# Weight casts put behind a stage's modulated tiles, and half of the sums of squares behind attention moved to Pool

## The chip, the cores and the metric

One core of one Trainium2 chip. The metric is the device time of one execution in microseconds (us); the median of three runs is given. The core's engines are TensorE (PE; its weight loads PEld), VectorE (DVE), ScalarE (ACT), Pool (POOL) and SyncE (SP, which issues the loads).

## The reference

Two token streams, 256 latent tokens and 256 context tokens of width 1024, go through two layers. A layer is: half feed-forward, a mixer, half feed-forward. Each block modulates its input with a shift and a scale that depend on a conditioning vector, and ends in a post-norm (residual times a constant, plus the gated output, then a layer norm). The mixer is attention in layer 0 and an mLSTM in layer 1; behind the mLSTM only the latents go on.

```python
def half_ffn(h, shift, scale, gate, w_in, w_out, g, b):
    xm = modulate(h, shift, scale)
    a, u = jnp.split(xm @ w_in, 2, axis=-1)
    y = (jax.nn.silu(a) * u) @ w_out
    return post_norm(h, 0.5 * gate * y, g, b)

for i in range(DEPTH):
    h_lat = half_ffn(h_lat, mod_lat[0], mod_lat[1], mod_lat[2], ...)
    h_ctx = half_ffn(h_ctx, mod_ctx[0], mod_ctx[1], mod_ctx[2], ...)
    xm_lat = modulate(h_lat, mod_lat[3], mod_lat[4])
    xm_ctx = modulate(h_ctx, mod_ctx[3], mod_ctx[4])
    o_lat, o_ctx = attention_mixer(...) if i % N_MIXERS == 0 else mlstm_mixer(...)
    h_lat = post_norm(h_lat, mod_lat[5] * o_lat, ln_g[i, 1], ln_b[i, 1])
    ...
```

## The kernel before, in words

The tokens lie along the free axis, the latents first (LAT, 0 to 256), the context behind them (CTX, 256 to 512); the width 1024 is eight tiles of 128 partitions. A product in nearly full precision is made of three matmuls (mm3): an operand is split into a rounded part and the low part that is left, and rounded x rounded, rounded x low and low x rounded are summed. split (line 225 on ScalarE, line 230 on VectorE) makes the two parts: ScalarE casts the number to its rounded part, then VectorE subtracts that from the number.

Weights come in chunks of 128 x 1024. chunk takes a raw buffer (three in rotation, in some stages one more), issues the load on SP's queue, takes one of seven pairs of buffers and splits. While the stage's function is being written out, a chunk stands where its unit first asks for it; a planner then orders the instructions of each engine by their readiness in its own model and keeps to data dependences, buffers, instructions pinned in order and edges that the kernel adds by hand. behind adds such an edge: if the fence has an entry for the instruction's engine, the instruction is to stand behind that entry's on this engine. Before the change only start uses it.

norm is a generator that writes a layer norm and the modulation of its result a step at a time, called by letters at chosen places: "b" or "B" begins one (latents or context), "m" makes the mean, eight "c" (line 478 subtracts the mean, line 485 squares on ScalarE, line 495 sums the squares), "v" the variance and the root (a chain of small instructions, lines 517 and 261 to 268, then line 521), "r" spreads the root over the partitions by a matmul (line 458, as are those of mean and variance), and eight "x" make the modulated tiles: line 551 on VectorE, the rounded part by line 552 on ScalarE, the low part by line 553 on VectorE. The tables LEADSTEP, ATTSTEP, MLSTEP, TAILSTEP and MTAILSTEP say after which unit and which k a letter is called. Line 495 sums on VectorE, but in the norm ahead of the last feed-forward (alone) on Pool for the tiles in POOLA.

A stage opens while the one before it ends: the norm of the latents is written in the tail of the earlier stage, that of the context in the first units of the new one, which work on the latents alone. In a feed-forward the first four units (LEAD) of two chunks each are first done for the latents, then for the context. In attention a unit is a block of 256 columns (part, two chunks, for one tile of 128 tokens; tokens 0 and 1 are the latents). In the mLSTM (jobs) a unit is one chunk: jobs 0 to 3 are queries and need the latents alone, job 4 the gates, jobs 5 to 8 the keys; jobs 0 to 6 (MLLEAD) are first done for the latents, then jobs 4 to 6 for the context, then 7 and 8 for both. Behind them come the value products (token_product, lines 969 to 971). The lines of the mLSTM that set the order are these:

```python
MLSTEP = {(1, 0): 'mcccccccc', (3, 5): 'v', (3, 7): 'rxxxxxxxx'}
MLLEAD = 7
...
            for n, (ws, i, to) in enumerate(jobs[:MLLEAD]):
                o = product(ws, i, LAT, None, lambda k: self.steps(MLSTEP.get((n, k), "")))
```

For the feed-forward LEADSTEP has the context's "v" at (2, 1) and "rxxxxxxxx" at (2, 5), for attention ATTSTEP has them at (3, 6) and (5, 0), with n counting the calls of part.

Of the kernel before, what the change touches and what calls it, by code (L numbers as in the profile page):

```python
# [54 lines left out]

LEAD = 4
TAIL = 4
ATTU = 4
# [55 lines left out]
FILL = (-1, -1, 1, 7)  # L114

POOLA = (0, 1, 2, 3, 4, 5, 6)
MAGIC = float(0x5F3759DF - (1 << 22))
# [54 lines left out]
class Body:  # L172
# [59 lines left out]
    def behind(self, ins):  # L232

        last = self.fence.get(ins.ins.engine)
        if last is not None:
            edge = mybir.DependencyInfo(mybir.DependencyClass.NoSync, mybir.DependencyReason.DATA)
            self.tc.add_manual_dep(ins.ins, last.ins.name, edge, reason="behind the start")

    def mm3(self, out, w, x, first, last, pin=False, group=True):
# [183 lines left out]

    seven = False

# [28 lines left out]
    def norm(self, g, coef, keep=True, nxt=True, alone=False):  # L454
# [20 lines left out]
        for d in range(ND):  # L475
# [10 lines left out]
            if alone and d in SQA:  # L486
                sums[d] = q, q
                continue
            eng = nc.gpsimd if alone and d in POOLA else V
            if eng not in sums:  # L490
# [51 lines left out]
        for d in range(ND):  # L542
# [8 lines left out]
            V.scalar_tensor_tensor(x, z, c[:, v, d : d + 1], rb[:, :w], ALU.mult, ALU.mult)  # L551
            S.activation(xh, x, AF.Identity, bias=e)  # L552
            V.scalar_tensor_tensor(self.xl[:, d, t0:t1], x, e, xh.bitcast(F32), ALU.add, ALU.subtract)
# [153 lines left out]
    def ffn(self, layer, s, gate, groups, side, start=None):  # L707
        nc, V = self.nc, self.nc.vector
        li = layer * 2 + s
        allg = BOTH  # L710
        call = lambda *k: side.get(k, lambda: None)()
        with self.tc.tile_pool(name=f"ffn{li}", bufs=1) as gp:
# [35 lines left out]
            for hf in range(2):  # L748
                js = list(range(hf * NFH, (hf + 1) * NFH))[0 if hf else done :]
                if hf == 0 and not start:  # L750
# [4 lines left out]
                    k0, k1 = range(ND // 2), range(ND // 2, ND)  # L755
                    for j in first[:-1]:
                        unit_in(j, ws[j], LAT, LEADSTEP[li])
                    j = first[-1]
# [8 lines left out]
                    for j in first:  # L767
                        call("in", j)
                    js = js[LEAD:]
                fast, sums = FAST[li]  # L770
# [203 lines left out]

    def attention(self, gate, side):
        nc, V, S, a = self.nc, self.nc.vector, self.nc.scalar, self.a
        with self.tc.tile_pool(name="att", bufs=1) as gp:
# [159 lines left out]
            for tiles in ((0, 1), (2, 3)):  # L1137
                assert len(self.running) == (tiles == (0, 1))
                for blk in range(3):
                    for tt in tiles:  # L1140
                        part(blk, tt, lambda k: self.steps(ATTSTEP.get((n, k), "")))
                        n += 1
                        if (blk, tt) == (2, 1):

                            for i in tiles:
                                part(3, i, ks=range(ND // 2))
                        if n > FINEATT:
                            self.fine = False
                        if blk == 1 and tt == tiles[1]:
                            done(n, 0, tiles, LAG + (tiles[0] > 0))  # L1150
                        turns(n)
            for tt in range(4):
                part(3, tt, ks=range(ND // 2 if tt < 2 else 0, ND))
# [66 lines left out]
    def mlstm(self, gate, side):  # L1220
        self.seven = True
        nc, V, S, a = self.nc, self.nc.vector, self.nc.scalar, self.a
        with self.tc.tile_pool(name="ml", bufs=1) as gp:
# [39 lines left out]
            outs = []  # L1263
            for n, (ws, i, to) in enumerate(jobs[:MLLEAD]):
                o = product(ws, i, LAT, None, lambda k: self.steps(MLSTEP.get((n, k), "")))
                if n < MH:
# [4 lines left out]
            for n, (ws, i, to) in enumerate(jobs):  # L1271
                if n < MH:
                    continue
                if n < MLLEAD:
                    o = product(ws, i, CTX, outs[n])
# [11 lines left out]
                if i >= MH - 2:  # L1287
                    w_v[0]((i - MH + 2) * ND)
            del w, w_q, w_g, ws, jobs
            wait = []  # L1290
            w_o = Keep(self, [a["ml_o"][i] for i in range(ND)], SH)
# [522 lines left out]
```

## Time and profile before

| | |
|---|---|
| time, median of 3 runs | 1612.9 us (1610.75 to 1613.86) |
| time of the profiled execution | 1613.07 us |
| its span, first to last instruction | 1611.2 us |
| TensorE busy | 1591.7 us, 99% |
| VectorE busy | 1369.2 us, 85% |
| ScalarE busy | 758.0 us, 47% |
| Pool busy | 30.6 us, 2% |
| mean granted clock of TensorE | 0.999 |

A time line of the trace gives the start in us from the first instruction, the time in us, engine and line, the operation with its shape and count, and in brackets the idle time of that engine just before and what ended it. A line of a helper (225, 230, 241) stands for all its callers, so places are told by their time.

### The profile page before, as it was taken

What the parts mean: (1) busy time and instruction counts of PE and PEld (TensorE: products, weight loads), DVE (VectorE), ACT (ScalarE), POOL (GpSimd) and SP (SyncE); (2) the same over time, 40 slices, a digit from 0 to 9 for tenths busy, and PEclk for the clock granted to TensorE, in tenths of its full rate; (3) what the DMA queues carried; (4) which work ended last, traced back from release to release, by engine and by line L of the source; (5) the groups of instructions that cost most, each with busy time, mean ns of one, the idle gap of its engine ahead of it and who ended that gap; (6) DMA issues with size and microseconds to landing.
All of it is one profiled execution on the core that took longest, in us unless ns stands there. A gap on an engine that the chain in (4) does not pass through costs nothing.

```text
span 1611.2 us, 26781 instructions
## 1 busy us (share of the span) xinstructions
PE 1591.7 (99%) x10364; PEld 1443.4 (90%) x10364; DVE 1369.2 (85%) x2790; ACT 758.0 (47%) x1342; POOL 30.6 (2%) x38
## 2 busy tenths in 40 slices
PE   9999999999999999999999999999999999999998
PEld 7888888889988998989999998889999889999986
DVE  7789989879878879689977989689977868897687
ACT  6522123215776444515652535326642757566542
POOL 0000000000011000000000000000000000020000
PEclk9999999999999999999999999999999999999999
DMA  9667877642203352542345252753363333527552
GB/s 361 219 209 225 260 229 243 218 133 86 66 1 105 106 157 67 196 157 105 105 171 183 79 179 70 253 179 106 131 203 112 112 118 92 161 101 262 184 170 92
DMA packets 72832, 250.02 MB, mean 155 GB/s; under 512 B 8952, under 2 KB 11768, under 8 KB 72704
## 3 DMA queue, kind: packets, MB, share of 16 engines
q1 hardware_dynamic: 70944, 246.99, 46.6%
q8 instruction: 81, 1.33, 0.3%
q10 hardware_dynamic: 1616, 0.79, 0.2%
q0 software_dynamic: 144, 0.52, 0.1%
q14 instruction: 47, 0.39, 0.1%
HBM read 247.22 MB, written 1.05 MB: 154 GB/s over the span
## 4 chain that ended last, share of the span: by engine, by line
PE 81%; DVE 10%; DMA 4%; ACT 3%; issue 1%; POOL 0%; DVEq 0%; ACTq 0%; SPq 0%; POOLq 0%
PE t L241 67%; PE t L1499 4%; DVE t L230 3%; PE t L969 2%; DMA t<-in_ffn_last 2%; PE t L970 2%; PE t L971 2%; ACT t L225 1%; DVE t L891 1%; PE t L897 1%; DMA t<-in_ffn_in 1%; DVE t L359 1%; DVE t L887 1%; DMA t<-in_ml_qk 1%; PE t L458 0%
## 5 line engine op out<-in xcount | busy, mean ns | idle before, releaser
L241 PE MATMUL t<-t,t 128*128 128x256 f32 (+2 forms) x8484 | 1299.0, 314 | 8.9 <-ACT t L552 4.2
L241 PEld LDWEIGHTS t<-t,t 128*128 128x128 f32 x8484 | 1175.4, 188 | 119.2 <-ACT t L552 5.2
L225 ACT CAST t<-t 128x512 fp32r<-128x512 f32 (+3 forms) x573 | 435.9, 785 | 507.6 <-PE t L241 187.0
L230 DVE TENSOR_TENSOR t<-t,t 128x256 fp32r<-128x256 f32 (+3 forms) x792 | 514.8, 686 | 95.4 <-ACT t L225 93.8
L359 DVE SCALAR_TENSOR_TENSOR t<-t,t 128x1024 bf16<-128x1024 f32 x224 | 260.5, 1219 | 0.2 <-DMA t<-in_ada_w 0.2
L741 DVE SCALAR_TENSOR_TENSOR t<-t,t,t 128x256 f32<-128x256 f32 x96 | 42.9, 478 | 46.0 <-PE t L241 45.8
L969 PE MATMUL t<-t,t 128*128 128x256 f32 (+1 forms) x256 | 78.8, 310 | 0.4 <-ACT t L552 0.4
L971 PE MATMUL t<-t,t 128*128 128x256 f32 (+1 forms) x256 | 78.4, 308 | 0.0
L970 PE MATMUL t<-t,t 128*128 128x256 f32 (+1 forms) x256 | 78.2, 307 | 0.0
L599 ACT ACTIVATE t<-t 128x256 f32<-128x256 f32 (+1 forms) x67 | 32.2, 483 | 93.7 <-PE t L241 92.4
L897 PE MATMUL t<-t,t 128*128 128x512 f32 (+1 forms) x300 | 60.8, 364 | 0.2 <-DVE t L891 0.2
L897 PEld LDWEIGHTS t<-t,t 128*128 128x128 f32 x300 | 51.4, 189 | 9.5 <-DVE t L891 0.6
L1499 PE MATMUL t<-t,t 128*128 128x512 f32 (+2 forms) x276 | 55.9, 358 | 0.0
L1499 PEld LDWEIGHTS t<-t,t 128*128 128x128 f32 (+1 forms) x276 | 45.0, 183 | 11.2 <-issue 1.5
L653 DVE TENSOR_TENSOR t<-t,t 128x512 f32<-128x512 f32 x78 | 53.5, 685 | 0.7
L969 PEld LDWEIGHTS t<-t,t 128*128 128x128 f32 x256 | 48.2, 189 | 3.3 <-ACT t L552 0.6
L970 PEld LDWEIGHTS t<-t,t 128*128 128x128 f32 x256 | 48.1, 188 | 2.7 <-DVE t L230 0.2
L971 PEld LDWEIGHTS t<-t,t 128*128 128x128 f32 x256 | 48.0, 188 | 2.5
L600 DVE TENSOR_TENSOR t<-t,t 128x256 f32<-128x256 f32 (+1 forms) x67 | 36.3, 544 | 16.1 <-ACT t L599 10.1
L552 ACT ACTIVATE t<-t,t 128x256 fp32r<-128x256 f32 x72 | 32.4, 502 | 37.3 <-DVE t L551 37.3
L890 ACT ACTIVATE t<-t,t 128x1024 fp32r<-128x1024 f32 x22 | 25.1, 1152 | 27.8 <-DVE t L888 26.5
L575 ACT ACTIVATE t<-t,t 128x256 f32<-128x256 f32 x64 | 29.7, 503 | 16.4 <-DVE t L574 16.4
(205 smaller groups left out, 1060.5 us busy)
## 6 DMA issues: line engine op xcount, KB each, us to landing
t<-in_ffn_in SPq DMA_DIRECT2D x168, 512.0 KB, 4.1
t<-in_ada_w SPq DMA_DIRECT2D x138, 512.0 KB, 4.4
t<-in_ffn_out SPq DMA_DIRECT2D x66, 512.0 KB, 4.5
t<-in_ffn_last SPq DMA_DIRECT2D x22, 512.0 KB, 3.7
t<-in_att_in SPq DMA_DIRECT2D x12, 512.0 KB, 3.7
t<-in_att_out SPq DMA_DIRECT2D x8, 512.0 KB, 3.5
t<-in_ml_qk SPq DMA_DIRECT2D x8, 512.0 KB, 4.5
t<-in_ml_v SPq DMA_DIRECT2D x8, 512.0 KB, 4.1
```

The source lines that it names most:

```text
L225: self.behind(self.nc.scalar.copy(h, x))
L230: self.behind(self.nc.vector.tensor_tensor(out=ls, in0=xs, in1=hs.bitcast(F32), op=ALU.subtract))
L241: mm = lambda *k, **kw: self.nc.tensor.matmul(*k, skip_group_check=not group, **kw)
L359: ins = nc.vector.scalar_tensor_tensor(self.tmp().bitcast(BF16), r, 1.0, self.cb[:, v, :], ALU.mult, ALU.mult, accum_out=to)
L600: V.tensor_tensor(out=sl, in0=sl, in1=pu[:, :n], op=ALU.mult)
L653: add = lambda o, x, y: V.tensor_tensor(out=o, in0=x, in1=y, op=ALU.add)
L741: V.scalar_tensor_tensor(z, y[:, gg[0] - t0 : gg[1] - t0], gate()[:, v, d : d + 1], z, ALU.mult, ALU.add)
L897: pin(nc.tensor.matmul(o, gs[g], ws[k][w][:, i : i + n], start=k == k0 and g == w == 0, stop=k == k1 - 1 and g == 1,))
L969: mm(o, self.xh[:, k, c], wh, start=k == 0, stop=False)
L970: mm(o, self.xh[:, k, c], wl, start=False, stop=False)
L971: mm(o, self.xl[:, k, c], wh, start=False, stop=k == ND - 1)
L1499: mm = lambda *k, **kw: pin(nc.tensor.matmul(*k, **kw))
```

## The change

A method hold_back sets the fence to ScalarE's last instruction of line 552 written so far. It is called in the feed-forward's first units ahead of the third unit, in attention ahead of the third block of the first two token tiles, in the mLSTM ahead of job 4 and again ahead of job 8; the fence is cleared at the end of each of these parts. While it is set, each cast that split writes is given an edge to that instruction. The fence has an entry for ScalarE alone, so the low parts on VectorE have none. Second, in the norm of the latents that attention's tail begins, line 495 sums the squares of tiles 2 to 5 on Pool, those of the others on VectorE.

```diff
--- before.py
+++ after.py
@@ -54,6 +54,7 @@
 FILLED = {6: (0, 1, 2), 7: (3, 4, 5)}
 
 LEAD = 4
+BACK = 2
 TAIL = 4
 ATTU = 4
 
@@ -113,6 +114,7 @@
 MLLEAD = 7
 FILL = (-1, -1, 1, 7)
 
+POOLD = (2, 3, 4, 5)
 POOLA = (0, 1, 2, 3, 4, 5, 6)
 MAGIC = float(0x5F3759DF - (1 << 22))
 
@@ -235,6 +237,9 @@
         if last is not None:
             edge = mybir.DependencyInfo(mybir.DependencyClass.NoSync, mybir.DependencyReason.DATA)
             self.tc.add_manual_dep(ins.ins, last.ins.name, edge, reason="behind the start")
+
+    def hold_back(self):
+        self.fence = {self.xlast.ins.engine: self.xlast}
 
     def mm3(self, out, w, x, first, last, pin=False, group=True):
         (wh, wl), (xh, xl) = w, x
@@ -421,7 +426,7 @@
         return ab, s, d
 
 
-    seven = False
+    seven = pooled = False
 
     def add_sum(self, g, d):
 
@@ -486,7 +491,7 @@
             if alone and d in SQA:
                 sums[d] = q, q
                 continue
-            eng = nc.gpsimd if alone and d in POOLA else V
+            eng = nc.gpsimd if d in (POOLA if alone else POOLD if self.pooled and g == LAT else ()) else V
             if eng not in sums:
                 sums[eng] = q, None
             else:
@@ -549,7 +554,7 @@
             xh = self.xh[:, d, t0:t1]
             e = e[:, v, d : d + 1]
             V.scalar_tensor_tensor(x, z, c[:, v, d : d + 1], rb[:, :w], ALU.mult, ALU.mult)
-            S.activation(xh, x, AF.Identity, bias=e)
+            self.xlast = S.activation(xh, x, AF.Identity, bias=e)
             V.scalar_tensor_tensor(self.xl[:, d, t0:t1], x, e, xh.bitcast(F32), ALU.add, ALU.subtract)
             if d == 1 and rs is not None and not raw:
                 S.copy(rs[:, :w], rb[:, :w])
@@ -706,6 +711,7 @@
 
     def ffn(self, layer, s, gate, groups, side, start=None):
         nc, V = self.nc, self.nc.vector
+        self.pooled = False
         li = layer * 2 + s
         allg = BOTH
         call = lambda *k: side.get(k, lambda: None)()
@@ -754,6 +760,8 @@
 
                     k0, k1 = range(ND // 2), range(ND // 2, ND)
                     for j in first[:-1]:
+                        if j == first[BACK]:
+                            self.hold_back()
                         unit_in(j, ws[j], LAT, LEADSTEP[li])
                     j = first[-1]
                     ps = unit_in(j, ws[j], LAT, ks=k0)
@@ -766,6 +774,7 @@
                         unit_in(j, ws[j], CTX)
                     for j in first:
                         call("in", j)
+                    self.fence = {}
                     js = js[LEAD:]
                 fast, sums = FAST[li]
                 w = Stream(self, [w_out[hf * NFH + i] for i in range(NFH)], lambda c, hf=hf: SHR if hf and c == (ND - TAIL) * NFH // ND else 0)
@@ -973,6 +982,7 @@
 
 
     def attention(self, gate, side):
+        self.pooled = True
         nc, V, S, a = self.nc, self.nc.vector, self.nc.scalar, self.a
         with self.tc.tile_pool(name="att", bufs=1) as gp:
             t = lambda shape, dt=F32, **k: self.t(shape, dt, pool=gp, **k)
@@ -1137,6 +1147,8 @@
             for tiles in ((0, 1), (2, 3)):
                 assert len(self.running) == (tiles == (0, 1))
                 for blk in range(3):
+                    if blk == BACK and tiles[0] == 0:
+                        self.hold_back()
                     for tt in tiles:
                         part(blk, tt, lambda k: self.steps(ATTSTEP.get((n, k), "")))
                         n += 1
@@ -1149,6 +1161,7 @@
                         if blk == 1 and tt == tiles[1]:
                             done(n, 0, tiles, LAG + (tiles[0] > 0))
                         turns(n)
+                self.fence = {}
             for tt in range(4):
                 part(3, tt, ks=range(ND // 2 if tt < 2 else 0, ND))
                 n += 1
@@ -1262,6 +1275,8 @@
             jobs = [(w_q, hd, qT) for hd in range(MH)] + [(w_g, 0, None)] + [(w, hd, kT) for hd in range(MH)]
             outs = []
             for n, (ws, i, to) in enumerate(jobs[:MLLEAD]):
+                if n == 2 * BACK:
+                    self.hold_back()
                 o = product(ws, i, LAT, None, lambda k: self.steps(MLSTEP.get((n, k), "")))
                 if n < MH:
                     conv(o, 1, i, qT[:, i, :])
@@ -1271,6 +1286,8 @@
             for n, (ws, i, to) in enumerate(jobs):
                 if n < MH:
                     continue
+                if n == MLLEAD + 1:
+                    self.hold_back()
                 if n < MLLEAD:
                     o = product(ws, i, CTX, outs[n])
                 else:
@@ -1287,6 +1304,7 @@
                 if i >= MH - 2:
                     w_v[0]((i - MH + 2) * ND)
             del w, w_q, w_g, ws, jobs
+            self.fence = {}
             wait = []
             w_o = Keep(self, [a["ml_o"][i] for i in range(ND)], SH)
 
```

## Rows read from the trace of the kernel before

**Rows 1.** the page: busy us (share of the span) xinstructions
```profile
PE 1591.7 (99%) x10364; PEld 1443.4 (90%) x10364; DVE 1369.2 (85%) x2790; ACT 758.0 (47%) x1342; POOL 30.6 (2%) x38
```

**Rows 2.** waits of TensorE: total us, times, longest us
```profile
PE t L241 <- ACT t L552: 4.2, 4, 1.2
```

**Rows 3.** TensorE's timeline, layer 1's first feed-forward: start, us, line, [idle before]
```profile
902.12 4.55 PE L241 MATMUL t<-t,t 128*128 128x256 f32 x37 [1.07 <-ACT t L552]
```

**Rows 4.** timeline of ScalarE, the same stretch
```profile
900.61 1.05 ACT L225 CAST t<-t 128x1024 fp32r<-128x1024 f32 x1 [1.60 <-DMA t<-in_ffn_in]
901.57 1.70 ACT L552 ACTIVATE t<-t,t 128x256 fp32r<-128x256 f32 x4
...
907.66 1.41 ACT L485 ACTIVATE t<-t 128x256 f32<-128x256 f32 x4 [2.53 <-DVE t L478]
```

**Rows 5.** timeline of TensorE, start of attention
```profile
382.38 0.38 PE L969 MATMUL t<-t,t 128*128 128x256 f32 x1 [0.39 <-ACT t L552]
```

**Rows 6.** timeline of TensorE, start of the feed-forward behind attention
```profile
551.42 1.44 PE L241 MATMUL t<-t,t 128*128 128x256 f32 x10 [1.20 <-ACT t L552]
```

**Rows 7.** timeline of VectorE, end of attention
```profile
543.02 0.41 DVE L495 TENSOR_TENSOR t<-t,t 128x256 f32<-128x256 f32 x1
```

**Rows 8.** timeline of ScalarE, end of attention
```profile
541.86 0.41 ACT L485 ACTIVATE t<-t 128x256 f32<-128x256 f32 x1
```

**Rows 9.** line 495 on VectorE and on Pool: ns min/median/max
```profile
L495 DVE TENSOR_TENSOR t<-t,t x56: 409/415/424, 367.1 to 1261.5; 128x256 f32<-128x256 f32 x56
...
L495 POOL TENSOR_TENSOR t<-t,t x6: 741/800/990, 1414.9 to 1419.8; 128x256 f32<-128x256 f32 x6
```

**Rows 10.** timeline of VectorE beside Pool's additions, ahead of the last feed-forward
```profile
1415.32 1.51 DVE L483 SCALAR_TENSOR_TENSOR t<-t,t,t 128x256 fp32r<-128x256 f32 x2
...
1421.01 0.47 DVE L483 SCALAR_TENSOR_TENSOR t<-t,t,t 128x256 fp32r<-128x256 f32 x1
```

**Rows 11.** timeline of ScalarE, start of the mLSTM
```profile
1246.03 1.05 ACT L225 CAST t<-t 128x1024 fp32r<-128x1024 f32 x1
...
1268.03 1.05 ACT L225 CAST t<-t 128x1024 fp32r<-128x1024 f32 x1 [4.29 <-DMA t<-in_ml_qk]
...
1272.50 1.05 ACT L225 CAST t<-t 128x1024 fp32r<-128x1024 f32 x1 [0.79 <-DMA t<-in_ml_qk]
1273.46 1.71 ACT L552 ACTIVATE t<-t,t 128x256 fp32r<-128x256 f32 x4
```

**Rows 12.** timeline of TensorE, start of the mLSTM
```profile
1250.15 3.80 PE L241 MATMUL t<-t,t 128*128 128x256 f32 x31 [0.99 <-ACT t L552]
...
1263.68 3.23 PE L241 MATMUL t<-t,t 128*128 128x256 f32 x26 [1.10 <-DVE t L230]
...
1267.21 5.89 PE L241 MATMUL t<-t,t 128*128 128x256 f32 x47
1274.01 18.02 PE L241 MATMUL t<-t,t 128*128 128x256 f32 x107 [0.92 <-ACT t L552]
1291.88 0.39 PE L969 MATMUL t<-t,t 128*128 128x512 f32 x1
```

**Rows 13.** timeline of VectorE, the context's root in the mLSTM
```profile
1262.63 0.16 DVE L517 TENSOR_SCALAR t<-t 128x2 f32<-128x2 f32 x1
...
1266.39 0.42 DVE L521 TENSOR_TENSOR t<-t,t 128x256 f32<-128x256 f32 x1
```

**Rows 14.** timeline of VectorE, the same steps unfilled, behind attention
```profile
568.46 0.16 DVE L266 TENSOR_TENSOR t<-t 128x2 f32<-128x2 f32 x1
568.65 0.16 DVE L267 SCALAR_TENSOR_TENSOR t<-t,t 128x2 f32<-128x2 f32 x1
```

**Rows 15.** stretches: length, PE busy (matmuls), PEclk, DMA, GB/s
```profile
1603.40:1607.40 4.00, 0.00 (x0) 1.00 0.00 0
1607.50:1611.20 3.70, 0.00 (x0) 0.50 0.39 144
```

**Rows 16.** timeline of SP's queue, start of the mLSTM
```profile
1264.47 0.33 SPq L210 DMA_DIRECT2D t<-in_ml_qk  x1
```

## The prediction

> **What bounds the kernel now.** I read the busy shares first: TensorE's matmuls fill 99% of the span and no other engine is near that [rows 1]. With one core and the matmuls one behind another, an edit can gain only what TensorE stands still, or lose by making it stand still. Second, the waits of TensorE: the largest entry, 4.2 us in four waits, is for ScalarE's line 552, the rounded part of a modulated tile, with which a stage opens [rows 2]. The span less TensorE's busy time is 19.5 us, 1.2% of the run, so no gain here can be large. Third, the timelines at the four places where a stage opens: latents into the feed-forward unit of layer 1, into attention, into the feed-forward unit behind attention, and into the mLSTM.
>
> The clearest is layer 1's first feed-forward. TensorE idles 1.07 us for line 552 until 902.12 [rows 3]. In ScalarE's timeline the reason stands just ahead: at 900.61 it runs a weight cast (line 225) whose load had landed only then (1.60 us idle for DMA), and the six waiting tiles follow from 901.57 [rows 4]. That cast belongs to unit 3; TensorE has units 0 to 2 to do first. ScalarE takes its instructions in order, so a cast that waits for a load holds tiles that are ready.
>
> **The change, part by part.** It has two mechanisms.
>
> *Casts behind the tiles in feed-forward and attention.* hold_back makes every later split's cast stand behind the last tile written by line 552 so far. In both feed-forward units it is called ahead of unit 2, when that is tile 7 of the latents (the context's tiles are emitted at (2, 5), later). In layer 1 the casts of chunks 4 to 6 move behind tile 7. They take 3 x 1.05 us and fill the 2.5 us in which ScalarE idled until 907.66 [rows 4], so they cost nothing; without that cover the context's squares would start about 1 us later. Their low parts, which free the raw buffers and so start SP's next loads, are already behind the tiles on VectorE; no load is later. Gain 1.2 us (the 1.07 of [rows 3] plus restart). Attention opens the same way: 0.39 us of waiting for line 552 [rows 5]; gain 0.5 us. Next late in both is the pace of VectorE's tile pairs, which TensorE does not outrun by more than a few tenths. Bounds for the two together: 0.5 to 2.0 us. Behind attention the casts that move keep no matmul waiting today; nothing.
>
> *Pool sums squares behind attention.* Of VectorE's seven additions (line 495) for the latents, four go, and Pool gets three; the variance takes two more one-column matmuls, under 0.3 us. The stage's stall is 1.20 us of idle until 551.42 [rows 6], at the end of the chain variance, root, spread, tile. The last addition starts at 543.02 [rows 7], but the last square ends at 541.86 + 0.41 [rows 8], so the variance can move forward by at most about 0.75 us, although four additions are up to 1.66 us. An addition takes 0.80 us on Pool against 0.415 on VectorE [rows 9]. The variance now waits for Pool too: its three additions can run from the fourth square on and end about with the last; nothing queues behind them, as Pool has 38 instructions in all [rows 1]. There is also a price: where Pool adds today, ahead of the last feed-forward, two VectorE instructions of line 483 took 1.51 us together, and the one behind them, without Pool beside it, 0.47 [rows 10]. That is an excess of 0.28 us for each, and I take it once per Pool addition: 0.85 lost against 1.66 leaves 0.8, about the 0.75 that the squares allow, and less the extra matmuls a gain of 0.5 us. Bounds: 1.1 us lost (three Pool additions block VectorE wholly, 2.4, and the extra 0.3 is paid, against 1.66) to 1.2 gained (the whole stall).
>
> The Trainium skill (SBUF — State Buffer, section "SBUF: two separate sides") speaks against this part: GpSimd and a VectorE instruction with two SBUF inputs share a port pair as an exclusive lock, the loser waiting for the whole instruction. Rows 10 agree in kind, though not in full length. By the rule taken to its end, the part loses the 1.1 us of the lower bound instead of gaining 0.5, and the sum is 1.6 us higher.
>
> *The mLSTM: the step that decides.* Here hold_back stands ahead of job 4, the gates. But MLSTEP emits the context's tiles, 'rxxxxxxxx', at (3, 7), inside job 3. So the last tile at that moment is the context's tile 7, not the latents'. The casts of jobs 4, 5 and 6 (gates and two key units), today from 1246.03 to about 1252, in the middle of the latents' tiles [rows 11], go behind an activation that ends at 1273.46 + 1.71 = 1275.2 [rows 11]. The second call, ahead of job 8, then adds nothing.
>
> Those three jobs are what TensorE does today while the context is normalised: 26 and 47 matmuls in the stretches from 1263.68 and 1267.21 [rows 12], 73 in all, where three units of 24 are 72. Behind the change it has nothing else: jobs 0 to 3 are done, their remaining products need the same weights, and the value products need loads whose buffers these casts hold. TensorE stands from the end of job 3, near 1260, to the first held-back cast.
>
> When does it go on? From 1275.2 I take off: 1.0 us, the latents' wait for line 552 at 1250.15, gone as in the other stages [rows 12]; 1.9 us, in which casts that wait for loads (1268.03, 1272.50) held the context's tiles [rows 11]; 1.5 us in the chain of the root, which runs 517 to 521 in 3.76 us, each small step filled up by a low part [rows 13], where unfilled steps follow at 0.19 us [rows 14] (eight are 1.6 us, with the convolutions some 2.2). That is 1270.8; one cast of 1.05 later, 1271.8; VectorE has one low part less ahead of the variance, so 1271.5. What then remains is the 73 matmuls (3.23 + 5.89 us), seven more of job 4 (0.8), and the unbroken work from 1274.01 to the first value product at 1291.88 (17.9) [rows 12]: about 27.6 without their tails, to 1299.0. So this stage ends 7.1 us later.
>
> To that comes the clock. In the last two stretches of the span, which have no matmul, the granted clock is 1.00 and then 0.50, 1.2 GHz [rows 15]. The hole, 11 us without work, is longer than both, so I expect the first matmuls behind it at the lower level. No row has matmuls at that level: bounds are nothing, and a whole unit (2.7 us) taking twice its time. I take 2.0 us. SP's three loads, issued today from 1264.47 [rows 16] as low parts free their buffers, come some 8 us later, but job 7 needs its weights only behind the 144 matmuls of jobs 4 to 6, over 16 us; ScalarE's and VectorE's queues behind the casts hold convolutions and gates that shift with TensorE. Bounds for the stage: 4.5 us lost (chain 2 us faster than I take it, no clock) to 12 (chain as late as today, full clock price).
>
> **Sum.** -1.2 - 0.5 - 0.5 + 7.1 + 2.0 = +6.9 us on the profiled execution's 1613.07 us, 0.2 above the median of 1612.9: 1620.0 us.
>
> **Rivals.** *No hole, faster.* If the edge is to the latents' tile, or the planned order still lets jobs 4 to 6 go early, the mLSTM gains instead: the wait until 1250.15 (0.99) and the one until 1274.01 (0.92) [rows 12], with restarts 2.2; total -1.2 - 0.5 - 0.5 - 2.2 = -4.4, 1608.7 us. For it speaks that a second call for job 8 would make sense only then; against it that the order of emission in MLSTEP is explicit and line 225 is fenced by engine. It turns on which tile is last at job 4. 12%.
> *Short hole, level.* If the context's chain, with VectorE and ScalarE freed of casts and low parts, ends near 1268.5 and the clock holds, the loss is 4.5 and the gains reach 3.5: 1614 us, within what can be told. Against it: eight tiles cost VectorE twelve instructions ahead of the last activation however free it is. 13%.
> *Long hole.* The context's chain is no faster than today: 1276.2 to go on, 11.8 us, with 2.7 for the clock 14.5; less 2.2: 1625.4. It is the upper end of my forecast, not counted apart.
>
> **How the numbers follow.** Slower by about 7 us: 75%, its own range 1615 to 1625.5. The measurement can tell 0.2%, 3.2 us, from no change. The forecast and its long end are slower; the short hole is the same; no hole is faster. For 8 in 10 the range takes the forecast and part of the short hole: 1611.5 to 1625.5.
>
> **What would show it.** Right: in the mLSTM stage the three casts stand behind the last eight line-552 activations; one idle piece of TensorE of 8 to 12 us ends with line 225, a clock below 1 behind it; the first value product comes 5 to 12 us later relative to the stage's first matmul. The waits near 902 and 382 are gone, three Pool additions of 0.8 us stand near 540. Wrong: casts of the gates ahead of the context's tiles, or matmuls of jobs 4 to 6 in the hole.

## The result, and the profile after

The changed kernel takes 1618.8 us (median of six runs, 1616.2 to 1620.3), the kernel before 1613.1 in the same session (six runs, 1610.8 to 1614.7): a ratio of 1.0036, 95% interval 1.0023 to 1.0049, or 5.7 us slower. The profiled execution is the fastest of the six, 1616.24 us with a span of 1614.4, so its whole is only 3.2 us above the profile before, and the change's cost has to be read in its stage. Line numbers have moved: the cast 225 is now 227, its low part 230 is 232, mm3 241 is 246, the norm's matmuls 458 are 463, the tile lines 551 to 553 are 556 to 558, 478/485/495 are 483/490/500, 517 is 522, 521 is 526, 969 is 978, and the 483 of [rows 10] is 488. Two lines of VectorE come up beside them: 435, now 440, adds to the running sum for the mean, and 958, now 965 (967 after the change), adds a gated matmul result, read from PSUM (the memory that matmuls write), to the residual.

The page's busy times and the longest waits of TensorE after the change (total us, times, longest us):

```profile
PE 1591.8 (99%) x10368; PEld 1444.4 (89%) x10368; DVE 1368.4 (85%) x2786; ACT 758.0 (47%) x1342; POOL 33.2 (2%) x41
```
```profile
PE t L246 <- ACT t L227: 8.1, 3, 7.2
PE t L463 <- DVE t L526: 1.8, 1, 1.8
```

TensorE's busy time is that of [rows 1]; its waits are others. The 4.2 us for the tile line [rows 2] are gone from the list, and in their place stand 7.2 us in one piece for a weight cast and 1.8 for the spread of the root. The place is the start of the mLSTM. TensorE's timeline there, after the change:

```profile
1256.71 0.74 PE L246 MATMUL t<-t,t 128*128 128x256 f32 x4 [0.51 <-DVE t L232]
1259.20 0.70 PE L463 MATMUL t<-t,t 128*128 128x256 f32 x2 [1.75 <-DVE t L526]
1267.07 29.75 PE L246 MATMUL t<-t,t 128*128 128x256 f32 x192 [7.17 <-ACT t L227]
1296.66 0.39 PE L978 MATMUL t<-t,t 128*128 128x512 f32 x1
```

The two waits come to 8.9 us. ScalarE's timeline at the first tile of the stage, before the change, and then of the stage after it:

```profile
1245.49 0.51 ACT L552 ACTIVATE t<-t,t 128x256 fp32r<-128x256 f32 x1 [5.74 <-DVE t L551]
```

```profile
1241.28 0.91 ACT L557 ACTIVATE t<-t,t 128x256 fp32r<-128x256 f32 x2 [5.74 <-DVE t L556]
...
1260.45 1.31 ACT L557 ACTIVATE t<-t,t 128x256 fp32r<-128x256 f32 x3 [2.89 <-DVE t L556]
1262.81 1.31 ACT L557 ACTIVATE t<-t,t 128x256 fp32r<-128x256 f32 x3 [1.05 <-DVE t L556]
...
1265.18 0.91 ACT L557 ACTIVATE t<-t,t 128x256 fp32r<-128x256 f32 x2 [0.60 <-DVE t L556]
1265.99 1.98 ACT L227 CAST t<-t 128x1024 fp32r<-128x1024 f32 x2
```

The casts of jobs 4 and 5 stand behind the context's eighth tile at 1265.99, and job 6's at 1268.19; before, they ran from 1246.03 on, among the latents' tiles [rows 11]. From the spread at 1259.20 until then TensorE has nothing. Two more things are to be read here. First, the context's chain is fast. The root's steps are no longer filled by low parts: from line 522 to line 526 they take 1.76 us, where they took 3.76 [rows 13]. VectorE's timeline shows it:

```profile
1256.96 0.15 DVE L522 TENSOR_SCALAR t<-t 128x2 f32<-128x2 f32 x1
...
1258.53 0.16 DVE L273 SCALAR_TENSOR_TENSOR t<-t,t 128x2 f32<-128x2 f32 x1
1258.72 0.42 DVE L526 TENSOR_TENSOR t<-t,t 128x256 f32<-128x256 f32 x1
```

Second, the clock. Stretches of the same stage (length, busy us of PE, PEld, DVE, ACT and POOL with their instructions, granted clock, DMA share, GB/s):

```profile
1250.00:1259.80 9.80, 7.25 (x53) 6.25 (x52) 8.84 (x33) 4.99 (x13) 0.00 (x0) 1.00 0.18 54
1259.80:1266.60 6.80, 0.10 (x1) 0.00 (x0) 6.66 (x17) 4.49 (x10) 0.30 (x1) 0.54 0.00 0
1266.60:1272.00 5.40, 4.93 (x28) 4.93 (x29) 4.57 (x14) 2.62 (x4) 0.00 (x0) 0.63 0.44 119
1272.00:1280.00 8.00, 8.00 (x71) 8.00 (x70) 4.59 (x4) 4.20 (x4) 0.00 (x0) 1.00 0.76 261
```

The hole has one matmul row in 6.8 us and the lower level (0.54 over the stretch); the first matmuls behind it still run at that level (0.63 over the stretch that holds them), 28 rows in 5.4 us, while the stretch after them has 71 in 8.0 us.

The other openings became faster. ScalarE at layer 1's first feed-forward, where a cast waited 1.60 us for its load in front of ready tiles [rows 4], and TensorE, whose wait of 1.07 us [rows 3] is gone:

```profile
898.11 1.31 ACT L557 ACTIVATE t<-t,t 128x256 fp32r<-128x256 f32 x3 [1.05 <-DVE t L556]
899.33 2.93 ACT L227 CAST t<-t 128x1024 fp32r<-128x1024 f32 x3
902.54 0.75 ACT L490 ACTIVATE t<-t 128x256 f32<-128x256 f32 x2 [0.28 <-DVE t L483]
```
```profile
892.93 8.61 PE L246 MATMUL t<-t,t 128*128 128x256 f32 x71
```

To put the gains and the loss side by side for all runs, I cut the run at the starts of tile-line instructions on ScalarE (552, later 557): **A** from the latents' first tile in attention to the context's; **B** from there to the latents' first tile in the feed-forward behind attention; **C** from the context's first tile there to the latents' first tile in layer 1's first feed-forward; **D** from there to its context's first tile; **E** from the latents' first tile in the mLSTM to the latents' first tile in the last feed-forward. All in us, one profiled execution each (names are those of the experiments below). How far one profile can be trusted is seen from e1 and e13, the same kernel twice: they differ by 0.12 in C, but by 0.76 in B and 0.86 in E. The kernel before had medians of 1612.6, 1613.5 and 1612.7 us in the three sessions of the experiments; the ratios below are each to that session's own. One execution each of the kernel before (first session), e2 and e3 took 2675 to 4931 us and is left out of the medians.

| | A | B | C | D | E | median of the runs |
|---|---|---|---|---|---|---|
| before | 21.03 | 151.96 | 325.61 | 22.60 | 187.89 | 1613.1 |
| after | 20.56 | 151.26 | 324.67 | 21.35 | 196.58 | 1618.8 |
| e1, e13 (fence at the latents) | 20.53, 20.54 | 151.03, 151.79 | 324.96, 325.08 | 21.34, 21.35 | 187.62, 188.48 | 1610.2, 1610.0 |
| e2 (no mLSTM fence) | 20.54 | 151.52 | 324.95 | 21.33 | 187.70 | 1610.1 |
| e3 (mLSTM fence alone) | 21.31 | 152.28 | 325.65 | 23.18 | 196.90 | 1622.3 |
| e4 (Pool alone) | 20.94 | 151.63 | 324.68 | 21.93 | 187.47 | 1610.6 |
| e5 (other fences alone) | 20.54 | 152.60 | 325.56 | 21.34 | 187.94 | 1610.6 |
| e6 (hole filled) | 20.54 | 151.26 | 324.66 | 21.34 | 195.57 | 1617.2 |
| e9 (e1 without Pool) | 20.44 | 151.75 | 325.80 | 21.34 | 187.58 | 1610.7 |
| e10 (fence from job 5) | 20.54 | 152.00 | 325.10 | 21.34 | 190.89 | 1611.7 |
| e11 (fence from job 6) | 20.55 | 151.59 | 325.03 | 21.34 | 187.38 | 1609.9 |
| e14 (Pool alone, one addition) | 20.84 | 152.38 | 325.35 | 21.98 | 189.25 | 1613.5 |

### The profile page after: what moved, and what is told of

The parts are those of the page before. It is cut to its first block, busy times and chain, and to the rows that moved or that the text cites. A ratio compares the mean times of both kernels' runs of the same rounds, so it can differ in the third digit from the quotient of the medians.

```text
span 1614.4 us, 26794 instructions
## 1 busy us (share of the span) xinstructions
PE 1591.8 (99%) x10368; PEld 1444.4 (89%) x10368; DVE 1368.4 (85%) x2786; ACT 758.0 (47%) x1342; POOL 33.2 (2%) x41
## 3 DMA queue, kind: packets, MB, share of 16 engines
HBM read 247.22 MB, written 1.05 MB: 154 GB/s over the span
## 4 chain that ended last, share of the span: by engine, by line
PE 86%; DVE 9%; ACT 3%; issue 1%; DMA 1%; POOL 0%; DVEq 0%; ACTq 0%; SPq 0%; POOLq 0%
PE t L246 70%; PE t L1517 4%; PE t L906 4%; DVE t L232 2%; PE t L978 2%; PE t L980 2%; PE t L979 2%; ACT t L227 1%; PE t L463 1%; DVE t L364 1%; DVE t L556 0%; ACT t L1079 0%; DMA t<-in_ffn_in 0%; DVE t L558 0%; DVE t L579 0%
```

## The experiments

**The fence's target in the mLSTM (e1), and no fence there (e2).** In e1 the last tile is kept before the loop, when it is still the latents'; the second call, ahead of job 8, stays:

```diff
+            lat = self.xlast
             for n, (ws, i, to) in enumerate(jobs[:MLLEAD]):
                 if n == 2 * BACK:
-                    self.hold_back()
+                    self.fence = {lat.ins.engine: lat}
```

> The mLSTM's fence at job 4 is the latents' last tile in place of the context's; all else as in the change. Theory (the loss is the hole that the context's tile makes): jobs 4 to 6 fill the context's norm again; from the first latent tile of the mLSTM to the first value product 43 to 46 us (46.4 before the change, 55.4 with it), clock near 1.00 throughout, and 1607 to 1610 us in all, as the gains of the other stages stay. Rival (Pool's use of the shared port, or the casts moved in the feed-forwards and attention, cost the time): still 1616 to 1620 us.

e2 leaves out both calls of hold_back in the mLSTM.

> Both calls in the mLSTM left out, all else as in the change. Theory: the mLSTM is as before the change (46.4 us from first latent tile to first value product), and the gains of the other stages alone are left: 1609 to 1611.5 us. Rival (cost outside the mLSTM): 1615 us or more.

e1 took 1610.2 us (ratio to before 0.9984, 0.9975 to 0.9992), e2 1610.1 (0.9985, 0.9976 to 0.9994). The tile that the edge points to turns 5.7 us lost into 2.5 gained; the granted clock has no dip left, and no piece of TensorE's idle time in the stage is above 1.6 us. So the loss is the hole, and the hole comes from the edge to the context's tile.

The stretch that the expectation of e1 names reads 39.46 us, below its 43 to 46, only because one row of the value products now stands ahead of the last key unit; to the second row of line 978 it is 46.96, against 47.22 in e2 and 56.06 after the change.

The fence on the latents' tile, though, gains nothing measurable over none: 1610.2 us against 1610.1, and 187.62 and 188.48 (e13) against 187.70 us in E. TensorE's timeline of e2, then of e1, in the stage:

```profile
1247.01 3.92 PE L246 MATMUL t<-t,t 128*128 128x256 f32 x31 [1.14 <-ACT t L557]
...
1260.64 3.23 PE L246 MATMUL t<-t,t 128*128 128x256 f32 x26 [1.10 <-DVE t L232]
...
1270.92 18.00 PE L246 MATMUL t<-t,t 128*128 128x256 f32 x107 [1.06 <-ACT t L557]
```
```profile
1257.28 3.69 PE L246 MATMUL t<-t,t 128*128 128x256 f32 x29 [1.18 <-DVE t L232]
...
1280.40 0.39 PE L978 MATMUL t<-t,t 128*128 128x512 f32 x1
1282.33 5.28 PE L246 MATMUL t<-t,t 128*128 128x512 f32 x22 [1.54 <-DVE t L232]
```

Both waits for tiles (1.14 and 1.06) are gone in e1, and a new one of 1.54 us stands ahead of the last key unit. Its load is issued at 1269.30, its cast runs at 1274.80, and its low part comes only at 1281.06, behind the gates' scans on VectorE; in e2 that load went out at 1264.83.

**The mLSTM fence alone (e3).** No hold_back in the feed-forward and in attention, no sums on Pool; the mLSTM as in the change.

> The two calls in the mLSTM alone; no fence in feed-forward and attention, no sums on Pool. Theory: the hole alone, 9 us more in the mLSTM stage: 1620.5 to 1623.5 us, slower than the change itself. Rival (cost outside the mLSTM): 1612 to 1614 us.

1622.3 us, ratio 1.0059 (1.0045 to 1.0072): some 9.5 us above the kernel before, 196.90 - 187.89 = 9.0 of it in E. TensorE again idles 1.75 us for the spread and 7.17 for the cast, the same two figures as after the change.

**The hole filled with other matmuls (e6).** Behind the spread's matmul ahead of job 4, 14 matmuls, 28 rows of the trace, are written into a buffer that nothing reads:

```diff
                     self.hold_back()
+                    fill = self.mm()
+                    for _ in range(14):
+                        self.pin(nc.tensor.matmul(fill[:, :TL], self.ident, self.h[:, 0, 0:TL], start=True, stop=True))
```

> The change, with 14 matmuls on unused data behind the spread of the root and ahead of job 4, which keep TensorE at work in most of the hole and write nothing that is read. Theory (part of the loss is the clock, which fell to 0.50 at 1260.4 and was back at 1270.6, 3.5 us after the matmuls went on at 1267.1): the clock stays at 1.00 and the time from the last tile's cast to the first value product is 1.8 us shorter: 1616.5 to 1617.5 us against 1618.8. Rival (the clock costs nothing there, VectorE's low parts or the casts set the pace): 1618 to 1619.5 us.

1617.2 us, ratio 1.0025 (1.0015 to 1.0035), 1.6 us below the change. The intervals of the two overlap, so this gain is read in the traces. The clock did not stay up, as the theory had it: the stretches show that it had fallen before the filling began.

```profile
1255.00:1258.00 3.00, 2.01 (x14) 1.53 (x14) 3.00 (x9) 1.63 (x4) 0.00 (x0) 1.00 0.00 0
1258.00:1262.00 4.00, 2.25 (x8) 1.77 (x8) 2.38 (x15) 0.42 (x1) 0.00 (x0) 0.55 0.43 131
1262.00:1266.00 4.00, 4.00 (x12) 3.21 (x12) 4.00 (x12) 2.91 (x7) 0.30 (x1) 0.60 0.00 0
1266.00:1270.00 4.00, 4.00 (x23) 3.59 (x23) 4.00 (x12) 3.39 (x7) 0.00 (x0) 1.00 0.02 6
```
```profile
1261.28 8.15 PE L1282 MATMUL t<-t,t 128*128 128x256 f32 x28
1269.08 27.59 PE L246 MATMUL t<-t,t 128*128 128x256 f32 x192
```

But it was back when the real matmuls went on, and so this run prices it: the same 192 rows take 27.59 us here and took 29.75 after the change, 2.2 us. Not all of that is the clock. The first 3.55 us of the 192, after the change and then in e6:

```profile
1267.07:1270.62 3.55, 3.55 (x16) 3.55 (x17) 3.55 (x12) 2.15 (x3) 0.00 (x0) 0.50 0.25 66
1269.08:1272.63 3.55, 3.55 (x32) 3.52 (x31) 3.55 (x11) 1.74 (x3) 0.00 (x0) 1.00 0.42 112
```

Up to the 24th row the difference is 1.6 us, and that is the lower level. The other 0.5 comes behind it, at a granted clock of 1.00: the 128x256 rows stand 118 ns apart after the change and 113 in e6. The kernel before has both spacings in this stage, and e3, with the same hole, has 113, so the 0.5 is not the hole's; its cause is open. Of the gain another 1.0 us is not seen in the time because the filling outlasts the hole: the 192 begin 26.75 us behind the latents' first tile, 25.79 after the change. So the time lies in the theory's range, but not in the way that the theory had it.

**Pool alone (e4) and the other fences alone (e5).** e4 leaves out all calls of hold_back; e5 has those of the feed-forward and of attention and sets pooled to False.

> Only the Pool sums of the change; no fence anywhere. Forecast's theory: the variance behind attention moves forward by what the squares allow, .75 us, less .3 for two more matmuls: gain 0.5 us, some 1612.2 us beside 1612.7 for the kernel before; the first tile (line 557) of the feed-forward behind attention comes about 0.5 us earlier after the first tile of the context in attention (before: 550.86 - 398.9 = 151.96 us). Rival, VectorE is blocked for the whole of each Pool addition: 1.1 us lost, 1613.8 us, first tile 153.1 us. Rival, VectorE loses nothing: the whole stall of 1.2 us goes, 1611.5 us, 150.8 us. In either case VectorE's instructions beside the three Pool additions are longer than without: by 0.28 us each for the forecast, by about 0.8 for the block.

> Only the fences in the feed-forward units and in attention; no Pool sums, no fence in the mLSTM. Forecast's theory: 1.2 us at layer 1's first feed-forward and 0.5 us at attention's opening, 1611.0 us beside 1612.7 for the kernel before; the wait of 1.1 us for the context's low part at the feed-forward behind attention (before 549.85 and 562.56) stays, since the casts moved there keep no matmul waiting. Rival, the casts moved behind attention matter too: that second wait goes here as well, a gain of 2.2 us or more, 1610.5 us, as much as the run without the mLSTM fences that had the Pool sums too. Rival, the waits only move further down: 1612.7 us.

Both took 1610.6 us (ratio 0.9981, 0.9972 to 0.9990, for each). Their medians can't be added up: each gains 3.0 us, the two together (e2) 2.4, and each interval is some 1.4 us wide to either side. The table separates them. The fences (e5) shorten A to 20.54 and D to 21.34, and leave C where it was, 325.56; Pool (e4) shortens C to 324.68. Without a fence D goes with the wait of a cast for its load: 22.60 before, where the cast waited 1.60 us for it, 23.18 in e3 (2.18 us), 21.93 in e4 and 21.98 in e14. Whether it is by chance that the two kernels with Pool sums have the shorter ones isn't shown. With a fence it is 21.33 to 21.35 in every run.

How Pool shortens C is not as forecast. From VectorE's first subtraction (line 483) to the variance (line 522) e4 takes 543.91 - 536.20 = 7.71 us, before it was 544.81 - 537.02 = 7.79. VectorE and Pool in e4:

```profile
536.20 1.42 DVE L483 TENSOR_TENSOR t<-t,t 128x256 f32<-128x256 f32 x4 [0.29 <-PE t L463]
...
539.18 0.48 DVE L965 SCALAR_TENSOR_TENSOR t<-t,t,t 128x256 f32<-128x256 f32 x1
539.95 0.97 DVE L500 TENSOR_TENSOR t<-t,t 128x256 f32<-128x256 f32 x1 [0.29 <-ACT t L490]
540.85 0.96 DVE L440 TENSOR_TENSOR t<-t 128x256 f32<-128x256 f32 x1
...
543.91 0.15 DVE L522 TENSOR_SCALAR t<-t 128x2 f32<-128x2 f32 x1
```
```profile
539.08 0.74 POOL L500 TENSOR_TENSOR t<-t,t 128x256 f32<-128x256 f32 x1 [35.58 <-ACT t L490]
539.90 0.74 POOL L500 TENSOR_TENSOR t<-t,t 128x256 f32<-128x256 f32 x1
540.72 0.81 POOL L500 TENSOR_TENSOR t<-t,t 128x256 f32<-128x256 f32 x1
```

Two of VectorE's instructions beside Pool's three additions take 0.97 and 0.96 us instead of 0.42, 1.1 us in all, and VectorE waits 0.29 for a square. Four additions fewer, on the other side, free only 1.3 us, since VectorE starts one every 0.33 us. So the variance comes only 0.08 earlier. What changed is TensorE's order. The statistics and the spread stand some ten matmuls earlier in it (from the mean's spread to the statistics the timeline counts 58 in e5, 48 in e4), and those ten fill the wait for the first tile. TensorE in e5 (no Pool sums), then in e4:

```profile
549.39 0.67 PE L463 MATMUL t<-t,t 128*128 128x256 f32 x2
551.25 1.32 PE L246 MATMUL t<-t,t 128*128 128x256 f32 x8 [1.19 <-ACT t L557]
...
562.98 0.97 PE L246 MATMUL t<-t,t 128*128 128x256 f32 x6 [0.49 <-DVE t L232]
564.10 1.80 PE L246 MATMUL t<-t,t 128*128 128x256 f32 x13 [0.16 <-DVE t L232]
```
```profile
542.20 1.05 PE L463 MATMUL t<-t,t 128*128 128x1 f32 x8 [0.39 <-DVE t L500]
...
548.73 0.59 PE L463 MATMUL t<-t,t 128*128 128x256 f32 x2
548.97 8.98 PE L246 MATMUL t<-t,t 128*128 128x256 f32 x68
```

The 1.19 us go, but 0.39 of waiting at the statistics and four more one-column rows (1.05 us for eight, 0.50 for four before; the forecast took two more and under 0.3) take most of their place: the first tile comes 13.74 us behind the first subtraction, before it was 13.84. What is left as gain is the second pair of waits, for low parts near 563, which e4 has not. By TensorE's waits alone that makes an estimate of 1.19 + 0.65 - 0.39 - 0.55 = 0.9 us.

**e1 without the Pool sums (e9), beside e1 once more (e13).** e9 differs from e13 in pooled alone.

> The run with the mLSTM's fence on the latents' tile, without the Pool sums. The run with the Pool sums alone showed the chain from the mean's spread to the latents' first tile behind attention unmoved (13.74 us from VectorE's first subtraction to line 557, 13.84 before), yet TensorE's wait of 1.2 us for that tile gone, and the wait of 0.6 us for a low part near 563 gone too; from the context's first tile of that feed-forward to layer 1's first latent tile it took 324.7 us, 325.6 without Pool. Theory: the Pool part is worth about 0.8 us, nearly all of it that second wait: here it is back, 325.5 to 325.7 us, and the time is 0.8 us above its twin with the Pool sums in this batch (about 1611.0 beside 1610.2). Rival, the medians are right and the Pool part is worth 3 us: 3 us above the twin.

> The change with the mLSTM's fence on the latents' last tile once more, unaltered, as the twin of the run without Pool sums on the same chip: 1610.2 us again, 2.5 below the kernel before, if the first measurement holds.

e9 took 1610.7 us (ratio 0.9988, 0.9979 to 0.9997), e13 1610.0 (0.9983, 0.9974 to 0.9992). The twins are 0.76 us apart, near the 0.9 of the waits, and e9 has the waits of 1.19, 0.49 and 0.16 us back and C at 325.80, so the rival of 3 us falls. But each interval is some 1.4 us wide to either side, so the medians alone do not set 0.76 apart from nothing. Nor does the difference in C measure it: 0.72, of which 0.28 is only a later start of C, since the context's first tile comes 20.17 us behind the latents' in e9 and 20.45 in e13; and the last feed-forward, with the same instructions in the same order in both, took 178.33 us in the one profile and 176.83 in the other. That e4 alone gained 3.0 is not explained by Pool's sums; about 0.7 of its profile is the earlier load in D, and the rest stays open within its interval.

**One Pool addition instead of three (e14).** As e4, with POOLD = (2, 3).

> Only the Pool sums, of tiles 2 and 3 alone: one Pool addition instead of three, and two of VectorE's instead of four go. Forecast's theory (VectorE's additions and the squares set the variance): about half of the three-addition run's effect. Theory from the traces: what counts is that the statistics get a second sum and stand some ten matmuls earlier in TensorE's order, so that matmuls of the old stage are left to fill the wait for the tile: the wait of 1.2 us for the first tile and that of 0.6 us for the low part near 563 are gone with one addition too, and the stretch from the context's first tile to layer 1's first latent tile is 324.7 to 325.0 us. Beside the one Pool addition VectorE loses about 0.5 us (0.97 and 0.96 for two additions of 0.42 beside three).

1613.5 us, ratio 1.0008 (0.9999 to 1.0017): nothing gained, which neither theory forecast. (The profiled execution is the slowest of its eleven, 1616.4 us.) The variance came earlier than in e4 (543.91 - 536.36 = 7.55 us behind the first subtraction) and the one disturbed addition took 0.77 us, yet from the variance to line 556 it took 6.14 us instead of 5.52, since in VectorE's order a line 965 that waits 0.89 us for TensorE stands between (0.24 in e4). In TensorE's order the statistics stand only five rows earlier than in e5 (53 behind the mean's spread, against 58 and e4's 48), so half of the wait for the tile is left, and the one for the low part is longer than before:

```profile
551.12 6.27 PE L246 MATMUL t<-t,t 128*128 128x256 f32 x48 [0.65 <-ACT t L557]
...
564.84 1.79 PE L246 MATMUL t<-t,t 128*128 128x256 f32 x13 [1.02 <-DVE t L232]
```

So the theory from the traces keeps its mechanism, rows that fill the wait, and fails in taking the order for given: the Pool part is worth what the order around it happens to be.

**Fences from job 5 (e10) and from job 6 (e11).** Both are e1 with the condition at a later job (e11 has + 2), and in place of the second call the fence is cleared at job 7:

```diff
-                if n == 2 * BACK:
+                if n == 2 * BACK + 1:
                     self.fence = {lat.ins.engine: lat}
...
-                if n == MLLEAD + 1:
-                    self.hold_back()
+                if n == MLLEAD:
+                    self.fence = {}
```

> The change, with the mLSTM's fence on the latents' last tile from job 5 on (the gates' cast of job 4 stays among the latents' tiles) and cleared behind job 6. The run with the fence on the latents' tile from job 4 on lost both waits for tiles in the mLSTM (1.1 us each in the run without mLSTM fences) and gained only 0.3 us, since a later wait of 1.5 us for the low part of the last key chunk took their place: its load was issued at 1269.30, 4.5 us later than without. Theory: that load is late because the gates' cast and low part, held back, free their raw buffer late; with job 4 left where it was the load is issued before 1267, the late wait is gone, and the stage from its first latent tile to the first value product is 45.5 us or less (46.5 without mLSTM fences): 1609.3 us. Rival, the load is late because of the casts of jobs 5 and 6: the late wait stays, 1610.2 us as with the fence from job 4 on.

> As the run with the fence from job 5 on, but from job 6 on, so that only one cast moves behind the latents' tile 7. In the run without mLSTM fences job 5's cast waited 0.97 us for its load and held the latents' tiles, job 6's 0.32 us. Theory that the wait of TensorE for the latents' tile (1.14 us) is job 5's cast waiting for its load: the wait stays, and the time is 1610.1 us or above, at most 0.3 better than without mLSTM fences (1610.4). Rival, it is the number of casts among the tiles: half of the wait goes, 1609.9 us.

e10: 1611.7 us (0.9988, 0.9979 to 0.9996), e11: 1609.9 (0.9979, 0.9970 to 0.9988). In e10 half of the theory held: the load of the last key chunk went out at 1263.76, as with no fence, and the wait on it is gone; whether job 4's cast or the missing second call freed it isn't shown, since e10 changes both. (The gain of 0.3 us that the expectation gives e1 over e2 isn't there: 1610.2 against 1610.1.) But the time did not follow, with E at 190.89 us. The next low part was late instead, that of a value chunk, behind the same scans:

```profile
1288.95 0.39 PE L978 MATMUL t<-t,t 128*128 128x512 f32 x1
1291.45 0.50 PE L979 MATMUL t<-t,t 128*128 128x512 f32 x1 [2.11 <-DVE t L232]
```

In e11 the wait for the latents' tile stayed, as expected (1.27 us, job 5's cast waiting 1.26 us for its load); its time can't be told from e1's, e2's or e13's. Every version without the fence on the context's tile, e14 apart, is 0.1 to 0.2% faster than the kernel before, with intervals that leave out 1; which of them is fastest the runs can't tell.

## Why the prediction was right, point by point

It was right in sign, in mechanism and nearly in size: +5.7 us where +6.9 was forecast.

- *The mLSTM, +7.1 and +2.0.* Right. The deciding step, that MLSTEP had emitted the context's tiles before hold_back was called, is shown by e1, which changes only the tile. Two signs of the forecast came out smaller: the idle time is 7.17 us in one piece and 1.75 ahead of the spread, where one piece of 8 to 12 was named, because TensorE ran until 1257.45, 16.2 us behind the latents' first tile, where 1260 was 14.5 behind it. TensorE was to go on at 1271.5 in the earlier kernel's time, 26.0 us behind the latents' first tile at 1245.49; it went on 25.8 behind (1267.07 - 1241.28). From that tile to the first value product it took 55.38 us where it was 46.39 before (1291.88 in [rows 12] less 1245.49), 9.0 more, against 9.1 forecast. The chain up to the casts was to be 4.7 us shorter and was 4.9: from the latents' first tile to the first subtraction 1.1 (1.0 was taken), on to the variance 0.4 (0.3), the root 2.0 (1.5), from there to the last tile's end 1.4 (1.9). So the close sum rests on terms that are each right to about half a us, with two of the misses in opposite directions, and unfilled steps at 0.19 us [rows 14] were the right rows for the largest. The clock's share was put at 2.0; e6 shows 1.6, and 0.5 of slower rows that no run ties to the hole. That the second call of hold_back adds nothing no run shows by itself.
- *Casts in the feed-forward and attention, -1.2 and -0.5.* Right, though of the "six waiting tiles" [rows 4] show four behind the cast; the last two came at 904.21, after a wait of 0.94 us for VectorE. D lost 1.25 us, A 0.47, in single profiles whose unfenced values scatter (D 21.93 to 23.18, A 20.84 to 21.31), and e5's C and B, no shorter than before, speak for it that the casts moved behind attention are worth nothing.
- *Pool, -0.5.* The sign held in the traces, the size by luck: 0.76 between the twins, 0.9 by the waits. The step that failed is "the variance can move forward by at most about 0.75 us", taken as a gain: the variance moved by 0.08, because two stretched VectorE instructions (1.1 us; 0.85 was taken) and a wait for a square took back what four additions gave, which was 1.3 us and not 1.66. The upper bound, "the whole stall", counted one stall and missed the second at 563, where the gain was made. The rule of an exclusive lock that the forecast weighed (the Trainium skill, SBUF — State Buffer, section "SBUF: two separate sides") would have lost 1.1 us taken to its end. The traces agree with the rule, and what was wrong is the 2.4 us: in e4 the two VectorE instructions with two SBUF inputs that began beside a Pool addition were held until 0.28 us behind its end (540.92 and 541.81, for additions that end at 540.64 and 541.53), while the one at 539.18, which reads one input from PSUM, took its usual 0.48. So VectorE lost what these two waited, 0.55 and 0.54 us, and not all of Pool's 2.4.
- *The rival without a hole, 1608.7.* e1 is that rival, at 1610.2 and 1610.0. Its price failed: 2.2 us were put on the two tile waits in the mLSTM, and nothing measurable came, because 1.54 us of waiting for a later low part took their place. What is late next was named for the other stages and not for this one.
- *The sum.* 1.2 us too slow: the stage costs 8.7 in E instead of 9.1, A, D and the twins give 2.5 instead of 2.2, and the rest is within what the medians can tell. The profiled pair alone would not show it: there E is 8.69 longer and A to D 3.39 shorter, but another 2.2 us went where the change does not reach, ahead of A and in the last feed-forward.

## What to carry to other kernels

An ordering edge is only as good as the instruction it points to when the line that sets it runs: look up what was emitted last at that moment, and what TensorE has to do until that instruction has run. When a wait is taken away, follow the freed work to the next buffer or queue before counting it, since here two removed waits of 1.1 us came back in large part as one of 1.5, and the time did not move. And where a planner orders the queues, a part's worth is in the order that comes out, so measure it against a twin that differs in that part alone.

## What the runs showed of the hardware that was not expected

The clock fell about as early as the hole began: 1.00 over the stretch to 1259.8, 0.54 over the next, and in e6 the lower level stood in the stretch from 1258, with 2.01 us of matmuls in the 3 us before it and the filling not begun before 1261.28. So a filling that starts behind the spread, the second part of the hole, came too late; one from the hole's start was not tried. In e10 the level fell behind its wait of 2.11 us, when the matmuls were already running again; the stretches of e10:

```profile
1289.40:1291.40 2.00, 0.00 (x0) 0.00 (x0) 1.94 (x4) 1.91 (x2) 0.00 (x0) 1.00 0.00 0
1291.40:1292.70 1.30, 1.25 (x5) 1.05 (x6) 1.30 (x2) 1.08 (x2) 0.00 (x0) 1.00 0.56 50
1292.80:1296.10 3.30, 3.30 (x10) 2.52 (x9) 2.30 (x4) 1.08 (x2) 0.00 (x0) 0.50 0.82 286
```

So a hole's clock price can stand away from the hole. Where Pool ran three additions back to back, which VectorE instruction is stretched goes by where it reads: those with two SBUF inputs that began while Pool added all ended 0.28 us behind that addition (five in e4, e14 and after the change), however long they had waited; lines 965 and 967, with one input from PSUM, took 0.48 us beside it. Ahead of the last feed-forward, where [rows 10] are from, it is the same in the kernel before: line 478, which reads the mean from PSUM, took 0.41 us beside Pool's additions, line 483 0.62 to 0.85. A fence also took scatter away: D is 21.33 to 21.35 us in the nine profiles with it, and 21.93 to 23.18 in the four without, where a load's landing decides.
